# Spreading the norm factors of a token pair by a DRAM store and a repeating load instead of by products

## The chip, the cores and the metric

The kernel runs on one core of one Trainium2 chip. The metric is the device time of one execution in microseconds (us), from launch to end. Before the change the median of three runs is 1037.97 us (1037.33 to 1039.09).

The engines are named as in the profile: PE is TensorE, DVE is VectorE, ACT is ScalarE, POOL is GpSimd, SP is SyncE, which here only issues DMAs. POOL can issue DMAs too; they form a queue of their own (q0 in the page of the profile, beside q1 of SP).

## What is computed

One layer of a hybrid decoder, for 2048 prompt tokens and 8 sample tokens of width 1024:

```python
def rmsnorm(x, g):
    y = x * lax.rsqrt(jnp.mean(x * x, axis=-1, keepdims=True) + NORM_EPS)
    return y * g

h = rmsnorm(x, norm_g)
p = h @ w_in                      # (tokens, 1024) @ (1024, 8 * 512)
rq, rk, rv, rg, hq, hf, hi, hgate = jnp.split(p, 8, axis=-1)
...                               # retention heads, HGRN2 heads, gates
y = x + concat(o_ret, o_hg) @ w_out
out = rmsnorm(y, final_norm_g)
```

All of it is float32. What matters here is the first line of the layer: each token's row of `x` is scaled by one number, its norm factor `rsqrt(mean(x*x) + eps)`. The kernel holds `x` transposed, with the 1024 features on the partitions and tokens along the free axis. There a token's factor has to stand on every partition, as a row, to be multiplied in.

## The kernel before, in words

The 2048 tokens are cut into 8 pairs of two 128-token chunks. The products of the first part (`v_pair`, line 393) go over the pairs three times, once for each set of weight columns (values, then rq and gates, then rk and gates). The list `TOK` (line 199) gives the pair of each of the 24 steps: 4, 5, 6, 7, 2, 3, 0, 1 in the first set, then 1, 2, 4, 5, 3, 6, 7, 0, then 0 to 7. Steps 0 and 1 are done in another way: plain products on unscaled tokens, scaled by the norm factors when they leave PSUM (`plain_out`, line 635, ACT, where the factor stands on the token's partition and needs no spreading). From step 2 on a pair is multiplied by seven products of sums of blocks (a Strassen-Winograd scheme, `CHAIN`, line 364), each of 12 matmuls 128x128 by 128x512 in a high and low split; a step is 84 such matmuls.

For step i, `tok_ops(i)` (line 306) makes the operands:
- eight DVE instructions (line 313) multiply the raw tokens `xr` by `norm_g` and by the spread factors, `spread_to[i]`, a tile of 128 partitions by 256 tokens named `rb`
- ACT and DVE split them into high and low parts (`hi_lo`, lines 115 and 116, tiles `ab_h` and `ab_l`)
- DVE forms the sums S1 to S4 (lines 328 to 331), which `s_split` splits (tiles such as `s20h`).
- The scaled tokens and sums are stored to DRAM (`a_dram`, `s_dram`). Later steps on the same pair read them back ("spooled"). Only steps 2 to 7, 10 and 11 scale raw tokens, because pairs 4 and 5, of the plain steps, are scaled when they come again.

The factors come from `stats`: `stats_load` (line 257) loads the untransposed tokens into tiles `xn` (two buffers, 256 KB each, on SP's queue), `stats_sum` (line 263) squares and sums them on ACT (line 267, four a pair), and `stats_end` (line 275) has POOL add the partial sums (line 277) and raise to -0.5 (lines 111 and 112) into `rs_all`, which has a chunk's 128 factors in one column, one on each partition.

Spreading is by product. `spread_dg(i)` (line 284) has DVE multiply the identity by each of the two columns (line 288, tile `dg`), `spread(i)` (line 290) has PE multiply an all-ones matrix by each of these diagonal matrices (line 293, PSUM tile `prs`; each of the two products shows as two matmuls in the trace) and DVE copy the result to `rb` (line 295). The sample tokens do the same on a small scale: `decode_dg` (line 620), `decode_spread` (line 623, tiles `prsd` and `rbd`), and a DVE instruction (line 628) that scales the sample tokens `xs`, which sit in the tile `pk`.

The order on PE is that of the program, written out by hand: `after[n]` lists what is issued behind product n of step i, `after[n - 0.5]` in its middle. On the other engines and in the queues of SP and POOL a list scheduler orders the instructions by its own estimate of when each can start, and takes what comes first in the program where several could. `behind(f)` (line 124) ties the instructions of `f` behind the last ones of DVE, ACT and SP at that place; `past` (line 300) ties `spread_dg` behind the DVE instructions of the pair's `tok_ops`. All engines and queues work through their own lists in order, so that an instruction that waits holds up those behind it.

In the start of the kernel (lines 644 to 715) the weights are loaded and split, `stats(0)`, `stats(1)` and `stats(2)` run, `spread_dg(2)` and `spread(2)` surround the last plain products, `tok_ops(2)` follows and `stats(3)`. In the loop (line 918) step i handles the rest of `stats(i + 2)`: squares of the first half at `after[2]`, of the second half at `after[4]`, while `spread_dg(i + 1)` stands at `after[0]` and `spread(i + 1)` at `after[1]`. In the steps 2 to 5 `wg_load` also loads 1 MB of raw weights (`wgr`) for the next set, which PE multiplies by the sample tokens (`wg_decode`, line 531, `pgd`, line 600) and DVE sums (`w_sums`).

Of the kernel before, what the change touches and what calls it, by code (L numbers as in the profile page):

```python
# [18 lines left out]
P = 128  # L19
# [4 lines left out]
NB = 8  # L24
# [17 lines left out]
def step_kernel(ctx, tc, a, out):  # L42
# [24 lines left out]
    dg_dram = dr.tile([8, NB, P], F32, tag="dg_dram", name="dg_dram")  # L67
    a_dram = [dr.tile([P, KT, 2 * P], F32, tag=f"a_dram{p}", name=f"a_dram{p}") for p in range(8)]
    s_dram = [dr.tile([2, P, 2, 4, P], F32, tag=f"s_dram{p}", name=f"s_dram{p}") for p in range(8)]
    w_sums_dram = [  # L70
        {op: dr.tile([P, 4, GW], F32, tag=f"ws{n}{op}", name=f"ws{n}{op}") for op in ("T1", "T2", "T3", "T4")}
        for n in range(3)
# [173 lines left out]
    def spooled(i):  # L246
        return i >= 2 * N_V or (i >= N_V and TOK[i] not in TOK[:2])
# [27 lines left out]
    def stats_end(i):  # L275
        p, ms = V_ORDER[i], st[i]
        pool.tensor_tensor(ms[:, 0:2], ms[:, 0:2], ms[:, 2:4], op=ALU.add)
        rsqrt_mean(rs_all[:, 2 * p : 2 * p + 2], ms[:, 0:2], D, EPS)

    spread_to = {}  # L280

    dgs = {}

    def spread_dg(i):
        t = vq.tile([P, GW], F32, tag="rk", name=f"dg{i}")
        dgs[i] = [t[:, :P], t[:, P : 2 * P]]
        for dg, c in zip(dgs[i], (2 * TOK[i], 2 * TOK[i] + 1)):
            dve.tensor_scalar(dg, ident, rs_all[:, c : c + 1], None, op0=ALU.mult)

    def spread(i):  # L290
        pt = ps_tr.tile([P, 2, P], F32, tag="tr", name=f"prs{i}")
        for j, dg in enumerate(dgs[i]):
            pe.matmul(pt[:, j], ones, dg, start=True, stop=True)
        dst = vq.tile([P, GW], F32, tag="rq", name=f"rb{i}")[:, :256]
        dve.tensor_copy(dst, pt.rearrange("p a b -> p (a b)"))
        spread_to[i] = dst

    sop, lows = {}, {}

    def past(i, f):  # L300
        if i not in lows:
            return f()
        with tc.issue_after(lows[i]):
            f()

    def tok_ops(i, held=None):
        store = held.append if held is not None else lambda f: f()
        r0, r1 = xr[i]
        for j, r in enumerate((r0, r1)):
            if not spooled(i):  # L310
                for k in range(4):
                    kk = 4 * j + k
                    dve.scalar_tensor_tensor(  # L313
                        r[:, k], r[:, k], g_in[:, kk : kk + 1], spread_to[i], op0=ALU.mult, op1=ALU.mult
                    )
# [8 lines left out]
        lows[i] = next(x for x in reversed(nc.cur_bb.bb.instructions) if x.engine == dve.engine)  # L324
# [293 lines left out]
    dgd = sm.tile([NB, NB], F32, tag="dgd", name="dgd", bufs=1)  # L618

    def decode_dg():  # L620
        dve.tensor_scalar(dgd, ident[:NB, :NB], rsd[:, 1:2], None, op0=ALU.mult)

    def decode_spread():
        pt = ps_tr.tile([P, NB], F32, tag="tr", name="prsd")
        pe.matmul(pt, ones[:NB, :], dgd, start=True, stop=True)
        rb = sm.tile([P, NB], F32, tag="rbd", name="rbd", bufs=1)
        act.activation(rb, pt, AF.Copy)
        dve.tensor_tensor(xs, xs, rb.unsqueeze(1).to_broadcast([P, KT, NB]), op=ALU.mult)

    def x_decode():  # L630
# [37 lines left out]
            wv_split(k)  # L668
    for k in (0, 4, 2, 6):
        tok_load0(1, k)  # L670
    stats(1)
    stats(2)
    decode_inputs()
    for k in range(KT):
        x_split0(1, k)
# [242 lines left out]
    for i in range(2, n_tok):  # L918
# [13 lines left out]
        if same(i + 1):  # L932
            for op in ("S1", "S2", "S3", "S4"):
                sop[i + 1, op] = sop[i, op]
        elif i + 1 < n_tok:
            if not spooled(i + 1):
                after[0] += [lambda i=i: past(i, lambda: spread_dg(i + 1))]
                after[1] += [lambda i=i: spread(i + 1)]
            tied = behind if i >= N_V - 1 else lambda f: f()
            late = 2 if same(i) else 0  # L940
            after[2 + late] += [
                lambda i=i, t=tied: t(lambda: tok_ops(i + 1)), lambda i=i, t=tied: t(lambda: s_split(i + 1, 0))
            ]
            after[4 + late // 2] += [lambda i=i, t=tied: t(lambda: s_split(i + 1, 1))]
        if i + 2 < n_tok and not same(i + 2):
# [1042 lines left out]
```

## Time and profile before

| | before |
|---|---|
| median of 3 runs | 1037.97 us |
| profiled execution | 1038.73 us |
| its span | 1037.0 us |
| PE busy | 1023.4 us, 99% |
| DVE busy | 746.6 us, 72% |
| ACT busy | 556.5 us, 54% |
| POOL busy | 129.0 us, 12% |
| moved by DMA | 255.61 MB, mean 247 GB/s |
| POOL's DMA queue (q0) | 7440 packets, 24.76 MB |

In the lines of the profile, a time such as 84.37 is the start in us from the start of the span and the number behind it the duration; a name on the left of `<-` is written, those on the right are read. A matmul's duration overlaps with the next one's, so what a matmul costs is read from the distance between starts, which is 0.23 us in a dense row of 128x512 products. "PEld" is the weight load ahead of a matmul. In brackets stands how long the engine had been idle and what released it. The lines of waits give the sum, the number of times and the longest, in us.

### The profile page before, as it was taken

How to read it: one execution, taken by the hardware profiler on the slowest of the kernel's cores; microseconds unless marked ns; L12 is line 12 of the kernel's file. 1: busy time of each engine (PE TensorE's matmuls, PEld its weight loads, DVE VectorE, ACT ScalarE, POOL GpSimd, SP SyncE). 2: the span in 40 equal slices, each digit the busy share in tenths (PEclk: the TensorE clock that was granted, in tenths of full speed). 3: DMA queues.
4: the chain of work that ended last, by engine and by line, in shares of the span. 5: the costliest groups of instructions: out<-in, count | busy, mean ns of one | idle time of the engine just before them, and what ended most of it. 6: DMA issues, size and time to landing. Idle time of an engine off the chain costs nothing. (4 is left out here: it accounts for less than half of the span.)

```text
span 1037.0 us, 21324 instructions
## 1 busy us (share of the span) xinstructions
PE 1023.4 (99%) x8231; PEld 849.9 (82%) x8231; DVE 746.6 (72%) x1387; ACT 556.5 (54%) x1217; POOL 129.0 (12%) x231
## 2 busy tenths in 40 slices
PE   9999999999999999999999999999999999999997
PEld 7777778887778888888888889898888878888775
DVE  6886676887666876666665767768768577667886
ACT  7863346644445765545554756566656465433232
POOL 0310001000000111111111100111012102311122
PEclk9999999999999999999999999999999999999999
DMA  8699999779998975586885686745783395575652
GB/s 295 217 326 327 341 326 314 272 250 328 316 333 295 374 241 162 161 276 210 238 256 163 244 313 225 257 138 187 230 266 122 118 370 203 178 271 190 238 184 102
DMA packets 151270, 255.61 MB, mean 247 GB/s; under 512 B 11424, under 2 KB 79280, under 8 KB 151040
## 3 DMA queue, kind: packets, MB, share of 16 engines
q1 hardware_dynamic: 143584, 229.22, 65.6%
q0 software_dynamic: 7440, 24.76, 6.2%
q8 instruction: 65, 1.06, 0.4%
q14 instruction: 37, 0.30, 0.1%
q10 hardware_dynamic: 144, 0.26, 0.1%
HBM read 166.51 MB, written 87.69 MB: 245 GB/s over the span
## 5 line engine op out<-in xcount | busy, mean ns | idle before, releaser
L1235 ACT ACTIVATE kepth<-kh 128x1024 f32<-128x1024 f32 x24 | 25.5, 1061 | 70.4 <-DVE kh L1225 70.4
L1039 PE MATMUL pjfh<-xh,w_h 128*128 128x512 f32 (+2 forms) x160 | 59.5, 372 | 0.0
L1039 PE MATMUL pjqh<-xh,w_h 128*128 128x512 f32 (+2 forms) x160 | 59.0, 368 | 0.0
L1039 PE MATMUL pjqh<-xh,w_l 128*128 128x512 f32 (+2 forms) x160 | 55.7, 348 | 0.0
L1039 PE MATMUL pjfh<-xl,w_h 128*128 128x512 f32 (+2 forms) x160 | 55.7, 348 | 0.0
L1039 PE MATMUL pjqh<-xl,w_h 128*128 128x512 f32 (+2 forms) x160 | 55.6, 347 | 0.1
L1039 PE MATMUL pjfh<-xh,w_l 128*128 128x512 f32 (+2 forms) x160 | 55.6, 348 | 0.0
L1225 DVE TENSOR_TENSOR kh<-kh,fph 128x512 f32<-128x512 f32 x48 | 33.3, 695 | 23.0 <-PE plh L1255 13.2
L116 DVE TENSOR_TENSOR ab_l<-xr,ab_h 128x512 fp32r<-128x512 f32 (+1 forms) x40 | 37.5, 954 | 7.1 <-ACT ab_h L115 6.8
L782 DVE SCALAR_TENSOR_TENSOR obr<-por,omr,rg 128x128 f32<-128x128 f32 x64 | 18.0, 344 | 32.4 <-POOL omr L774 32.4
L772 ACT ACTIVATE obr<-por 128x128 f32<-128x128 f32 x64 | 16.9, 278 | 43.2 <-PE por L759 40.9
L115 ACT ACTIVATE ab_h<-xr 128x512 fp32r<-128x512 f32 (+1 forms) x40 | 32.4, 840 | 13.6 <-DVE xr L313 13.6
L419 ACT ACTIVATE vo<-vo 128x512 f32<-128x512 f32 x32 | 20.1, 630 | 27.3 <-DVE vo L413 13.4
L1039 PEld LDWEIGHTS pjqh<-xh,w_h 128*128 128x128 f32 x160 | 30.4, 190 | 4.6 <-issue 1.2
L1039 PEld LDWEIGHTS pjfh<-xh,w_h 128*128 128x128 f32 x160 | 30.2, 189 | 4.1 <-issue 0.4
L1039 PEld LDWEIGHTS pjqh<-xh,w_l 128*128 128x128 f32 x160 | 30.1, 188 | 4.2 <-issue 0.3
L1039 PEld LDWEIGHTS pjfh<-xh,w_l 128*128 128x128 f32 x160 | 30.1, 188 | 4.0
L1228 DVE TENSOR_TENSOR qqh<-qqh,fph 128x512 f32<-128x512 f32 x48 | 32.8, 684 | 0.0
L1039 PEld LDWEIGHTS pjqh<-xl,w_h 128*128 128x128 f32 x160 | 30.2, 189 | 2.9
L1039 PEld LDWEIGHTS pjfh<-xl,w_h 128*128 128x128 f32 x160 | 30.2, 189 | 2.7
L313 DVE SCALAR_TENSOR_TENSOR xr<-xr,g_in,rb 128x256 f32<-128x256 f32 x64 | 27.1, 480 | 7.1 <-issue 4.3
L1666 PE MATMUL py<-woh,oc_h 128*128 128x512 f32 x64 | 26.7, 417 | 0.0
(1840 smaller groups left out, 3383.1 us busy)
## 6 DMA issues: line engine op xcount, KB each, us to landing
xr<-a_dram SPq DMA_DIRECT2D x24, 512.0 KB, 5.2
S<-s_dram SPq DMA_DIRECT2D x24, 512.0 KB, 5.8
xn<-in_x_prompt SPq DMA_DIRECT2D x32, 256.0 KB, 3.5
xr<-in_x_t SPq DMA_DIRECT2D x16, 512.0 KB, 5.7
a_dram<-xr SPq DMA_DIRECT2D x16, 512.0 KB, 4.1
s_dram<-S SPq DMA_DIRECT2D x16, 512.0 KB
wgr<-in_w SPq DMA_DIRECT2D x16, 512.0 KB, 8.3
xr<-a_dram SPq DMA_DIRECT2D x32, 256.0 KB, 4.4
```

Source lines behind the costliest of these rows:

```text
L115: act.activation(h, src, AF.Copy)
L116: dve.tensor_tensor(l, src, h.bitcast(F32), op=ALU.subtract)
L313: dve.scalar_tensor_tensor(r[:, k], r[:, k], g_in[:, kk : kk + 1], spread_to[i], op0=ALU.mult, op1=ALU.mult)
L419: act.activation(o, src, AF.Silu)
L772: act.activation(o[:, cc], po[:, h], AF.Square, scale=P ** -0.5, accum_out=ms[:, h : h + 1])
L782: dve.scalar_tensor_tensor(o[:, cc], po[:, h], ms[:, h : h + 1], rb_of[c, "g"][:, cc], op0=ALU.mult, op1=ALU.mult)
L1039: pe.matmul(ps, ww[:, kk], x[:, k, b0 : b0 + n], start=(k == 0 and i == 0), stop=(k == KT - 1 and i == 2),)
L1225: dve.tensor_tensor(kv[:, :, 0, :], kv[:, :, 0, :], two[:, :, 1:2].to_broadcast([P, nb, b]), op=ALU.mult)
L1228: dve.tensor_tensor(qv[:, :, 1, :], qv[:, :, 1, :], two[:, :, 0:1].to_broadcast([P, nb, b]), op=ALU.mult)
L1235: act.activation(ss[:, 512:], k[:, :HALF], AF.Copy)
L1666: pe.matmul(ps, o[:, kk], w[:, k % 4, i * 512 : (i + 1) * 512], start=(k == 0 and n == 0), stop=(k == KT - 1 and n == 2),)
```

## The change

- `stats_end` stores the pair's 256 factors to DRAM, `rs_dram`, by a DMA of POOL's queue. For a pair of step 2 or later it calls `spread(i)` at once.
- `spread(i)` becomes one DMA on POOL's queue, which reads the 1 KB of factors 128 times over and writes them to all partitions of `rb`. It needs no PE, no PSUM and no DVE. `spread_dg` is gone, the tiles of `rb` alternate between the buffers `rq` and `rk`.
- For steps 10 and 11, whose factors lie in DRAM since the start, `spread` is issued behind product 4 of the step two ahead.
- All `stats` move one pair ahead: step i handles `stats(i + 3)`, `stats(4)` is in the start, and `stats(2)` comes before `stats(1)`. Their number does not change.
- `decode_spread` becomes a store and a repeating load on POOL's queue as well. The scaling of the sample tokens is a function of its own, `decode_scale`.

```diff
@@ tensors
+    rs_dram = [dr.tile([2, P], F32, tag=f"rs_dram{p}", name=f"rs_dram{p}") for p in range(8)]
+    rsd_dram = dr.tile([1, NB], F32, tag="rsd_dram", name="rsd_dram")
@@ stats_end
         rsqrt_mean(rs_all[:, 2 * p : 2 * p + 2], ms[:, 0:2], D, EPS)
+        pool.dma_start(rs_dram[p].rearrange("c t -> t c"), rs_all[:, 2 * p : 2 * p + 2])
+        if i >= 2:
+            spread(i)
@@
-    def spread_dg(i):
-        t = vq.tile([P, GW], F32, tag="rk", name=f"dg{i}")
-        dgs[i] = [t[:, :P], t[:, P : 2 * P]]
-        for dg, c in zip(dgs[i], (2 * TOK[i], 2 * TOK[i] + 1)):
-            dve.tensor_scalar(dg, ident, rs_all[:, c : c + 1], None, op0=ALU.mult)
-
     def spread(i):
-        pt = ps_tr.tile([P, 2, P], F32, tag="tr", name=f"prs{i}")
-        for j, dg in enumerate(dgs[i]):
-            pe.matmul(pt[:, j], ones, dg, start=True, stop=True)
-        dst = vq.tile([P, GW], F32, tag="rq", name=f"rb{i}")[:, :256]
-        dve.tensor_copy(dst, pt.rearrange("p a b -> p (a b)"))
+        dst = vq.tile([P, GW], F32, tag=("rq", "rk")[i % 2], name=f"rb{i}")[:, :256]
+        pool.dma_start(dst, rs_dram[TOK[i]].rearrange("c t -> (c t)").partition_broadcast(P))
         spread_to[i] = dst
@@ sample tokens
-    def decode_dg():
-        dve.tensor_scalar(dgd, ident[:NB, :NB], rsd[:, 1:2], None, op0=ALU.mult)
-
     def decode_spread():
-        pt = ps_tr.tile([P, NB], F32, tag="tr", name="prsd")
-        pe.matmul(pt, ones[:NB, :], dgd, start=True, stop=True)
         rb = sm.tile([P, NB], F32, tag="rbd", name="rbd", bufs=1)
-        act.activation(rb, pt, AF.Copy)
+        pool.dma_start(rsd_dram.rearrange("o b -> b o"), rsd[:, 1:2])
+        pool.dma_start(rb, rsd_dram[0].partition_broadcast(P))
+        dec_rb.append(rb)
...
+    def decode_scale():
+        rb = dec_rb[0]
         dve.tensor_tensor(xs, xs, rb.unsqueeze(1).to_broadcast([P, KT, NB]), op=ALU.mult)
@@ start
+    stats(2)
     stats(1)
-    stats(2)
...
-    spread_dg(2)
...
             if (c, ty) == (0, 0):
-                spread(2)
                 held = []
                 tok_ops(2, held)
...
     s_split(2, 1)
-    stats_load(4, 0)
+    stats(4)
+    stats_load(5, 0)
@@ loop, step i
-            if not spooled(i + 1):
-                after[0] += [lambda i=i: past(i, lambda: spread_dg(i + 1))]
-                after[1] += [lambda i=i: spread(i + 1)]
...
+        if N_V <= i + 2 < 2 * N_V and not spooled(i + 2):
+            after[4] += [lambda i=i: spread(i + 2)]
-        if i + 2 < N_V:
-            after[1 if i == 2 else 2] += [lambda i=i: behind(lambda: stats_sum(i + 2, 0)), lambda i=i: stats_load(i + 2, 1)]
-            after[4] += [lambda i=i: behind(lambda: stats_sum(i + 2, 1)), lambda i=i: stats_end(i + 2)]
-            if i + 3 < N_V:
-                after[5] += [lambda i=i: stats_load(i + 3, 0)]
+        if i + 3 < N_V:
+            after[1 if i == 2 else 2] += [lambda i=i: behind(lambda: stats_sum(i + 3, 0)), lambda i=i: stats_load(i + 3, 1)]
+            after[4] += [lambda i=i: behind(lambda: stats_sum(i + 3, 1)), lambda i=i: stats_end(i + 3)]
+            if i + 4 < N_V:
+                after[5] += [lambda i=i: stats_load(i + 4, 0)]
...
         if i == 2:
             after[3] += [lambda: behind(decode_values_out)]
-            after[0] += [decode_dg]
-            after[2] += [decode_spread]
+            after[0] += [decode_spread]
+            after[2] += [decode_scale]
```

More of the change, by code (lines that the diff above doesn't have):

```diff
@@ L278, in stats_end @@
         rsqrt_mean(rs_all[:, 2 * p : 2 * p + 2], ms[:, 0:2], D, EPS)
+        pool.dma_start(rs_dram[p].rearrange("c t -> t c"), rs_all[:, 2 * p : 2 * p + 2])
+        if i >= 2:
+            spread(i)
     spread_to = {}
-    dgs = {}
-    def spread_dg(i):
-        t = vq.tile([P, GW], F32, tag="rk", name=f"dg{i}")
-        dgs[i] = [t[:, :P], t[:, P : 2 * P]]
-        for dg, c in zip(dgs[i], (2 * TOK[i], 2 * TOK[i] + 1)):
-            dve.tensor_scalar(dg, ident, rs_all[:, c : c + 1], None, op0=ALU.mult)
-    def spread(i):
-        pt = ps_tr.tile([P, 2, P], F32, tag="tr", name=f"prs{i}")
-        for j, dg in enumerate(dgs[i]):
-            pe.matmul(pt[:, j], ones, dg, start=True, stop=True)
-        dst = vq.tile([P, GW], F32, tag="rq", name=f"rb{i}")[:, :256]
-        dve.tensor_copy(dst, pt.rearrange("p a b -> p (a b)"))
-        spread_to[i] = dst
[L298 to L304, printed above, removed]
+    def spread(i):
+        dst = vq.tile([P, GW], F32, tag=("rq", "rk")[i % 2], name=f"rb{i}")[:, :256]
+        pool.dma_start(dst, rs_dram[TOK[i]].rearrange("c t -> (c t)").partition_broadcast(P))
+        spread_to[i] = dst
+    sop = {}
     def tok_ops(i, held=None):
@@ L323, in tok_ops @@
             return
-        lows[i] = next(x for x in reversed(nc.cur_bb.bb.instructions) if x.engine == dve.engine)
         a11, a21, a12, a22 = r0[:, :, :P], r0[:, :, P:], r1[:, :, :P], r1[:, :, P:]
@@ L616, in decode_values_out @@
             sp.dma_start(vd_dram[ty], t)
-    dgd = sm.tile([NB, NB], F32, tag="dgd", name="dgd", bufs=1)
-    def decode_dg():
-        dve.tensor_scalar(dgd, ident[:NB, :NB], rsd[:, 1:2], None, op0=ALU.mult)
     def decode_spread():
-        pt = ps_tr.tile([P, NB], F32, tag="tr", name="prsd")
-        pe.matmul(pt, ones[:NB, :], dgd, start=True, stop=True)
         rb = sm.tile([P, NB], F32, tag="rbd", name="rbd", bufs=1)
-        act.activation(rb, pt, AF.Copy)
+        pool.dma_start(rsd_dram.rearrange("o b -> b o"), rsd[:, 1:2])
+        pool.dma_start(rb, rsd_dram[0].partition_broadcast(P))
+        dec_rb.append(rb)
+    dec_rb = []
+    def decode_scale():
+        rb = dec_rb[0]
         dve.tensor_tensor(xs, xs, rb.unsqueeze(1).to_broadcast([P, KT, NB]), op=ALU.mult)
```

## The prediction, made before the result was known

> **What bounds the kernel now.** I read the page first, then the busy time by stage, then the PE rows around the removed products, then PE's waits, then the rows of the other engines between 34 and 64 us, where the first pair to be scaled is prepared.
>
> The page:
>
> ```profile
> span 1037.0 us, 21324 instructions
> PE 1023.4 (99%) x8231; PEld 849.9 (82%) x8231; DVE 746.6 (72%) x1387; ACT 556.5 (54%) x1217; POOL 129.0 (12%) x231
> ```
>
> PE is busy for all but 14 us. So an instruction that leaves PE's list shortens the kernel by what it took there, unless PE then waits at that place or soon behind it; and work taken off DVE or ACT is worth nothing by itself. The profiled execution took 1038.73 us for this span, so 1.73 us lie around it, which the change doesn't touch.
>
> The products that go, from a dense place (PE's rows in order of time):
>
> ```profile
> 84.37 0.61 PE L293 MATMUL prs<-dg,ones 128*128 128x128 f32 x4
> 84.74 0.47 PE L360 MATMUL pv3a<-T2h,s30h 128*128 128x512 f32 x1
> 85.05 0.39 PE L360 MATMUL pv3a<-T2l,s30h 128*128 128x512 f32 x1
> 85.28 0.40 PE L360 MATMUL pv3a<-T2h,s30l 128*128 128x512 f32 x1
> ...
> 66.35 0.38 PE L625 MATMUL prsd<-dgd,ones 8*128 8x8 f32 x2
> 66.66 0.50 PE L360 MATMUL pv2c<-T1h,s21h 128*128 128x512 f32 x1
> 67.00 0.40 PE L360 MATMUL pv2c<-T1l,s21h 128*128 128x512 f32 x1
> ```
>
> Starts of neighbouring 128x512 products lie 0.23 us apart (85.05 to 85.28). One spread holds PE from 84.37 to 84.74, 0.37 us, and the product behind it starts late by a further 0.31 - 0.23 = 0.08 us: 0.45 us for a spread. The sample tokens' spread costs 0.31 + (0.34 - 0.23) = 0.42 us.
>
> How many there are, by the groups of that line (a spread is four of them):
>
> ```profile
> L293 PE MATMUL prs<-dg,ones x32: 272/274/275, 49.9 to 227.9; 128*128 128x128 f32 x32
> ```
>
> So eight spreads, all before 228 us.
>
> Second, the places where PE stands still near them. In the rows of PE when the first scaled pair begins (`pv2a`):
>
> ```profile
> 55.60 0.39 PE L360 MATMUL pv<-wv_h,ab_l 128*128 128x512 f32 x1
> ...
> 57.61 0.39 PE L360 MATMUL pv2a<-wv_l,ab_h 128*128 128x512 f32 x1
> ...
> 59.68 0.39 PE L360 MATMUL pv2b<-wv_l,ab_h 128*128 128x512 f32 x1
> ...
> 60.64 0.40 PE L360 MATMUL pv2b<-wv_h,ab_h 128*128 128x512 f32 x1
> ...
> 62.71 0.61 PE L293 MATMUL prs<-dg,ones 128*128 128x128 f32 x4
> 63.42 0.50 PE L360 MATMUL pv2a<-T2h,s20h 128*128 128x512 f32 x1
> ```
>
> From 55.60 to 57.61 there are five starts, which take 1.14 us where nothing waits, so 0.87 us are lost; from 59.68 to 60.64 there are two, 0.50 us lost. Behind the spread at 62.71 the next product comes after 0.71 us and not 0.37, 0.34 us lost. PE waits here for the operands of step 2, 1.7 us in all. From PE's list of waits there is one more:
>
> ```profile
> PE pgd L600 <- DMA wgr<-in_w: 1.0, 2, 0.5
> ```
>
> Twice, 0.5 us each, the sample tokens' products wait for raw weights, in a stretch where the DMA engines are full (busy time by stage; behind the clock come the DMA engines' busy share and GB/s):
>
> ```profile
> 64.00:85.00 21.00, 21.00 (x106) 16.49 (x105) 16.14 (x30) 9.74 (x20) 1.84 (x3) 1.00 0.99 371
> 85.00:107.00 22.00, 21.51 (x108) 16.80 (x108) 16.00 (x28) 9.06 (x17) 1.08 (x3) 1.00 0.96 334
> 107.00:128.00 21.00, 21.00 (x107) 16.56 (x106) 15.16 (x27) 9.29 (x17) 1.08 (x3) 1.00 0.98 343
> 128.00:150.00 22.00, 21.51 (x108) 16.87 (x107) 15.07 (x26) 9.25 (x17) 1.08 (x3) 1.00 0.95 343
> ```
>
> **The change part by part.** *Products removed:* 8 x 0.45 + 0.42 = 4.0 us off PE.
>
> *What of it comes back as waiting.* The spread at 62.71 stands in front of a wait: if the operand `s20h` and the freed bank come no sooner, PE only waits 0.45 us longer there. In the full DMA stretch PE comes to `pgd` sooner by each spread left out, while the weights come when DMA brings them; of the two places that wait, I count one as giving its 0.45 us back. (The second lies in step 5, which loses its 1 MB of `xn`, since all squares are one step earlier; that relief is worth more than the 128 KB that a repeating load adds.) That makes 4.0 - 0.9 = 3.1 us.
>
> *The way of the factors for step 2.* This is what is new and tight. POOL's rows, and the DVE and ACT rows that follow from them:
>
> ```profile
> 34.57 4.94 POOL L277 TENSOR_TENSOR ms<-ms 128x2 f32<-128x2 f32 x1 [6.81 <-ACT xn L267]
> ...
> 39.87 0.71 POOL L112 TENSOR_TENSOR rs_all<-rs_all,mhalf 128x2 f32<-128x2 f32 x1
> ...
> 56.39 1.18 POOL L112 TENSOR_TENSOR rs_all<-rs_all,mhalf 128x2 f32<-128x2 f32 x1
> ```
>
> ```profile
> 50.54 0.42 DVE L295 COPY rb<-prs 128x256 f32<-128x256 f32 x1 [1.79 <-PE prs L293]
> 51.00 2.47 DVE L313 SCALAR_TENSOR_TENSOR xr<-xr,g_in,rb 128x256 f32<-128x256 f32 x6
> ```
>
> ```profile
> 55.02 0.63 ACT L267 ACTIVATE xn<-xn 128x512 f32<-128x512 f32 x1 [1.36 <-DMA xn<-in_x_prompt]
> ...
> 55.65 0.61 ACT L115 ACTIVATE ab_h<-xr 128x512 fp32r<-128x512 f32 x1
> ```
>
> Before, `rb` of step 2 is there at 50.96, because PE reaches the spread so late. After, `stats(2)` takes the slot of `stats(1)`, whose factors are ready at 39.87 + 0.71 = 40.58. Then come a store and a repeating load. Neither is in this trace; the nearest rows are POOL's DMA issues and the times to landing:
>
> ```profile
> L575 POOL DMA_DIRECT2D T1l<-ws1T x2: 540/540/540, 171.9 to 173.2; - x2
> ```
>
> ```profile
> d_dram<-de POOLq DMA_DIRECT2D x8, 2.0 KB, 1.9
> ...
> o_dram<-obr POOLq DMA_DIRECT2D x16, 256.0 KB, 4.5
> ...
> out_new_hgrn_prompt<-S POOLq DMA_DIRECT2D x4, 64.0 KB, 3.0
> ...
> do<-d_dram POOLq DMA_DIRECT2D x1, 32.0 KB, 5.8
> ...
> dv<-vd_dram SPq DMA_DIRECT2D x8, 512.0 KB, 8.7
> ```
>
> The store moves 1 KB in pieces of 4 bytes. It is nearest to the 2 KB one in size, to the 256 KB one in the number of pieces: 1.9 to 4.5, I take 3.2. The load writes 128 KB; the only load by POOL from a small DRAM tensor took 5.8, a POOL store of 64 KB 3.0, and the repeating load that SP issues, of four times the size, 8.7. I take 5.8, the row nearest in kind, and the other two for bounds. With two issues of 0.54: 40.58 + 0.54 + 3.2 + 0.54 + 5.8 = 50.7, bounds 46.6 and 54.9. So the factors come about when they came before. Six scalings take 2.47 us, so four, which the first `ab_h` needs, 1.65. That `ab_h` started at 55.65, not because of DVE but because ACT stood before a square that waited for `xn`. Up to `rb` at 55.65 - 1.65 = 54.0 nothing changes; behind that each us is lost on PE, so the upper bound costs 0.9. The lower one can win the 1.7 us of waiting, if ACT's list lets `ab_h` ahead of the squares. I take zero.
>
> [...]
>
> *The wait on POOL's queue.* The load waits for the store to land, and behind it in POOL's list stand the adds and powers of `stats(1)`, whose factors `plain_out` uses on ACT. If they slip by 2 to 3 us, so does an emptying of PSUM whose bank PE needs again only for `pv2b`, seen at 59.68, which is a cover of over 10 us: nothing for PE; ACT's squares behind it wait for `xn` anyway.
>
> *Later steps.* Step 3's factors are ready at 57.57, by the same 10.1 us its `rb` is there at 67.7, the first `ab_h` could run at 69.4, and PE needs it only behind step 2's last product:
>
> ```profile
> 76.21 0.39 PE L360 MATMUL pv2a<-T4h,ab_h 128*128 128x512 f32 x1
> ```
>
> Seven us are left. From step 4 on the factors are a whole step earlier, 84 products of 0.23 us. Steps 10 and 11 have them in DRAM. Cost zero. The 9 stores and 9 loads are POOL time at 12% busy; DVE loses the diagonals, the copies and its waits for factors, ACT keeps its 32 squares. Zero each.
>
> *Sum:* -3.1 us. The profiled execution would be 1035.6; it lies 0.76 above the median of the runs, so the median goes from 1037.97 to 1034.9. A difference of 0.2%, 2.1 us, is about what can be told from none here (the three runs lie within 1.8). The forecast has bounds of -2.2 (upper bound of `rb`) and -4.0 (nothing comes back).
>
> **The rivals.** *First: the start clears too.* `rb` comes at 47 to 48, DVE is free then, and the first `ab_h` goes ahead of the late squares. Then the 1.7 us of waiting and the 0.45 at 62.71 are won: -3.1 - 2.1 = -5.2, 1032.8. For it: nothing ties `rb` to PE any more. Against: the 5.8 row, and ACT's order.
>
> *Second: DMA holds the pace from step 2 to 5.* The spreads of steps 2 to 5, the one at 62.71 among them, each stand ahead of a `pgd`. If all four times 0.45 end as waits for weights, 4.0 - 1.8 = 2.2 is left; with the 0.35 us of DMA time that 128 KB take at 371 GB/s added at the two places that wait already, 1.5: 1036.5. For it: the two `pgd` waits. Against: PE waits nowhere else there.
>
> *Third, on the other side: squares in front of the first operands on ACT.* The start has `stats(4)` whole, untied, where its first half used to be tied behind step 2. A square costs:
>
> ```profile
> L267 ACT ACTIVATE xn<-xn x32: 612/620/633, 17.4 to 144.0; 128x512 f32<-128x512 f32 x32
> L267 ACT ACTIVATION_READ_ACCUMULATOR xn<-xn x32: 184/187/191, 17.9 to 144.5; 128x1 f32 x32
> ```
>
> ```profile
> ACT xn L267 <- DMA xn<-in_x_prompt: 5.3, 7, 1.4
> ```
>
> That is 0.81 of work and 5.3 / 7 = 0.76 of waiting for `xn`, 1.57 us. Four squares before 55.65 already make PE wait. Two more ahead of step 2's splits cancel the gain (-3.1 + 3.1: 1038.0), four turn it to +3.2: 1041.2. It decides from two on. For it: the scheduler fills ACT's gaps by its own guess of when `xn` lands. Against: in the program `stats(4)` stands behind step 2's splits.
>
> *Fourth: POOL is held up by DVE.* The add at 34.57 took 4.94 us, the median of its line is 0.22:
>
> ```profile
> L277 POOL TENSOR_TENSOR ms<-ms x8: 195/224/4942, 24.8 to 144.8; 128x2 f32<-128x2 f32 x8
> ```
>
> DVE ran two-input instructions without a gap all that time. If the two DMA issues are held as long, `rb` comes 2 x 4.7 later, at 60.1, 6.1 us past the 54.0: -3.1 + 6.1 = +3.0, 1041.0; from 57.1 on the gain is gone. [...] Against it for DMAs: the issues of line 575 took 0.54 us.
>
> **How the numbers follow.** Forecast 0.42; start clears 0.17; DMA holds the pace 0.19; squares in front 0.09 with two, 0.07 with four; POOL held up 0.06. Faster by over 0.2%: 0.42 + 0.17 = 0.59. Within: 0.19 + 0.09 = 0.28. Slower: 0.07 + 0.06 = 0.13. The time is the forecast's, 1034.9. The range leaves out the two slower cases (0.13) and the far end of the first rival: 1032.3 to 1038.9. The faster cases alone span 1032.3 to 1035.8.
>
> **What would show it.** Right: no line with `prs` or `prsd`; PE busy lower by 3 to 4 us; the POOL queue up by 18 transfers; the first scaling of step 2 near 51; PE waits before `pv2a` and `pv2b` of 1 to 2 us. The first rival shows as these waits gone, the second as `pgd` waits of over 2 us, the third as squares waiting for `xn` ahead of `ab_h` and `s20h`, the fourth as long POOL issues between 40 and 50. The forecast is wrong if PE loses more than 3 us before 64, or if any later step waits for `rb`.

## The result, and the profile after

The changed kernel takes 1107.8 us (median of 4 runs, 1105.0 to 1113.0) against 1037.7 for the kernel before (four runs): a ratio of 1.067 (95% interval 1.064 to 1.069), 70 us slower. The forecast was 1034.9 with a range to 1038.9; direction and size are both wrong. The profiled execution took 1109.16 us.

The page of the changed kernel; PE's busy share, the granted clock (PEclk), both in tenths, and GB/s are given for 40 equal slices of the span:

```profile
span 1107.4 us, 21244 instructions
...
PE 1042.6 (94%) x8197; PEld 855.4 (77%) x8197; DVE 741.4 (67%) x1362; ACT 557.2 (50%) x1216; POOL 139.3 (13%) x249
...
PE   9946489999999999999999998999999999999997
...
PEclk9967889999999999999999998999999999999999
...
GB/s 289 144 164 181 152 347 266 279 371 170 313 316 332 313 337 277 176 176 242 213 226 263 157 269 249 200 279 160 137 290 175 154 222 320 97 342 157 242 174 96
...
q0 software_dynamic: 8144, 25.82, 6.8%
```

The clock and GB/s of the kernel before:

```profile
PEclk9999999999999999999999999999999999999999
...
GB/s 295 217 326 327 341 326 314 272 250 328 316 333 295 374 241 162 161 276 210 238 256 163 244 313 225 257 138 187 230 266 122 118 370 203 178 271 190 238 184 102
```

From the second to the fifth slice (28 to 138 us) the DMA engines moved about half as much as before, and from the third to the sixth, in which PE was busy for four to eight tenths, the granted clock was six to eight tenths. PE's busy time did not fall by 4 us, it rose by 19: the same matmuls ran longer. The start of each step on PE shows how much was lost where (min/median/max ns, then the first and last start in us). The changed kernel:

```profile
L347 PE MATMUL pv2a<-wv_h,ab_h x4: 392/628/793, 63.1 to 66.7; 128*128 128x512 f32 x4
...
L347 PE MATMUL pv3a<-wv_h,ab_h x4: 395/396/396, 111.8 to 113.9; 128*128 128x512 f32 x4
...
L347 PE MATMUL pv4a<-wv_h,ab_h x4: 395/396/396, 155.6 to 157.7; 128*128 128x512 f32 x4
...
L347 PE MATMUL pv5a<-wv_h,ab_h x4: 395/396/396, 179.7 to 181.8; 128*128 128x512 f32 x4
```

The kernel before:

```profile
L360 PE MATMUL pv2a<-wv_h,ab_h x4: 389/391/497, 56.3 to 58.8; 128*128 128x512 f32 x4
...
L360 PE MATMUL pv3a<-wv_h,ab_h x4: 389/389/389, 78.9 to 81.0; 128*128 128x512 f32 x4
...
L360 PE MATMUL pv4a<-wv_h,ab_h x4: 389/389/389, 100.4 to 102.4; 128*128 128x512 f32 x4
...
L360 PE MATMUL pv5a<-wv_h,ab_h x4: 389/389/389, 121.2 to 123.2; 128*128 128x512 f32 x4
```

Step 2 starts 7 us late, step 3 by 33, step 4 by 55, step 5 by 58.5. The rest, some 12 us, comes later. The rows also show a second thing: the undisturbed matmul takes 396 ns instead of 389.

Why the steps start late is seen on POOL. In the changed kernel line 281 is the store, line 289 the repeating load, line 114 the power that ends the making of the factors:

```profile
42.15 1.20 POOL L114 TENSOR_TENSOR rs_all<-rs_all,mhalf 128x2 f32<-128x2 f32 x1
43.65 0.79 POOL L281 DMA_DIRECT2D rs_dram<-rs_all  x1 [0.30 <-POOL rs_all L114]
54.05 0.58 POOL L289 DMA_DIRECT2D rb<-rs_dram  x1 [9.62 <-DMA rs_dram<-rs_all]
...
88.14 0.72 POOL L114 TENSOR_TENSOR rs_all<-rs_all,mhalf 128x2 f32<-128x2 f32 x1
89.27 0.80 POOL L281 DMA_DIRECT2D rs_dram<-rs_all  x1 [0.41 <-POOL rs_all L114]
99.55 0.57 POOL L289 DMA_DIRECT2D rb<-rs_dram  x1 [9.48 <-DMA rs_dram<-rs_all]
```

POOL waits 9.6 us for a store of 1 KB, and 9.5 for the next that it reads back. The first scaling of steps 2, 3 and 4 on DVE follows:

```profile
60.09 0.88 DVE L301 SCALAR_TENSOR_TENSOR xr<-xr,g_in,rb 128x256 f32<-128x256 f32 x2
...
103.86 2.46 DVE L301 SCALAR_TENSOR_TENSOR xr<-xr,g_in,rb 128x256 f32<-128x256 f32 x6 [19.57 <-DMA rb<-rs_dram]
...
133.92 2.46 DVE L301 SCALAR_TENSOR_TENSOR xr<-xr,g_in,rb 128x256 f32<-128x256 f32 x6 [16.12 <-DMA rb<-rs_dram]
```

Steps 3 and 4 wait for `rb`. At step 2 `rb` had landed at about 58 (54.05 and 3.9 to landing), and DVE came to the scaling late from a wait for a split on ACT, which in its turn had stood 1.33 us for the factors of pair 1.

And the DMA issues (KB each, median us to landing); the `xn` loads took 3.5 us before:

```profile
xn<-in_x_prompt SPq DMA_DIRECT2D x32, 256.0 KB, 8.9
...
rb<-rs_dram POOLq DMA_DIRECT2D x8, 128.0 KB, 6.1
...
rs_dram<-rs_all POOLq DMA_DIRECT2D x8, 1.0 KB, 10.2
```

So the repeating load costs what was thought (6.1 for 5.8, single ones from 3.3 to 10.1), and the store three times as much (10.2 for 3.2). That alone would make `rb` late. But `xn` is loaded by another queue, and the change added nothing to those loads: what made them land 5 us later?

### The profile page after: what moved, and what is told of

Same layout as the page of the kernel before. It is cut to its first block, busy times and chain, and to the rows that moved or that the text cites. A ratio compares the mean times of both kernels' runs of the same rounds, so it can differ in the third digit from the quotient of the medians.

```text
span 1107.4 us, 21244 instructions
## 1 busy us (share of the span) xinstructions
PE 1042.6 (94%) x8197; PEld 855.4 (77%) x8197; DVE 741.4 (67%) x1362; ACT 557.2 (50%) x1216; POOL 139.3 (13%) x249
## 4 chain that ended last, share of the span: by engine, by line
PE 61%; DMA 4%; DVE 3%; ACT 1%; issue 1%; SPq 0%; POOLq 0%; POOL 0%; ACTq 0%
PE po L347 11%; PE pjfh L1024 7%; PE pjqh L1024 7%; PE py L1651 4%; PE plh L1240 1%; PE par L730 1%; PE pur L737 1%; PE por L743 1%; PE por L745 1%; DMA or<-o_dram 1%; PE puh L1111 1%; PE poh L1127 1%; PE pv21a L347 1%; PE pv22a L347 1%; PE pv19a L347 1%; PE pv16a L347 1%
## 5 line engine op out<-in xcount | busy, mean ns | idle before, releaser
L768 DVE SCALAR_TENSOR_TENSOR obr<-por,omr,rg 128x128 f32<-128x128 f32 x64 | 18.0, 344 | 32.5 <-POOL omr L760 27.8
L269 ACT ACTIVATE xn<-xn 128x512 f32<-128x512 f32 x32 | 19.9, 624 | 34.2 <-DMA xn<-in_x_prompt 34.1
```

Of the source, the lines that this page charges most:

```text
L269: act.activation(r, r, AF.Square, accum_out=st[i][:, 2 * h + j : 2 * h + j + 1])
L768: dve.scalar_tensor_tensor(o[:, cc], po[:, h], ms[:, h : h + 1], rb_of[c, "g"][:, cc], op0=ALU.mult, op1=ALU.mult)
```

## The experiments

**The theories.** Theory 1: the store in 256 pieces of 4 bytes takes about 10 us and holds up every other transfer meanwhile. Rival A: the new order of the squares. Rival B: the repeating load of 128 KB. A third theory came with the 396 ns: where the operands lie. Each run's ratio is to the kernel before, run on the same chip, with its 95% interval. "Pair n" here and in the expectations is the pair of step n. Where rows of the input or of ones are spread, the expectation says so; their times are of the same work with other numbers.

**The stores alone** (e2): the kernel before plus the stores, which nothing reads. The order of the instructions on SP, ACT and DVE stays that of before, line for line; this holds for e5, e7, e8, e11, e13 and e16 as well.

```diff
 rsqrt_mean(rs_all[:, 2 * p : 2 * p + 2], ms[:, 0:2], D, EPS)
+pool.dma_start(rs_dram[p].rearrange("c t -> t c"), rs_all[:, 2 * p : 2 * p + 2])
```

> The kernel before, with one addition: the eight 1 KB stores in 256 pieces of 4 B, right behind each pair's factors on GpSimd. Nothing reads them; products, squares and their order stay as they were. Theory 1: 40 to 70 us slower than before (1078 to 1108), the xn loads at 8 to 9 us to landing, and a wait of ScalarE for xn of 5 us and more behind each early store. Rivals A and B: 1037 to 1040, since the order stays and there is no repeating load; nothing waits for the stores.

Measured: 1078.1 us, ratio 1.039 (1.037 to 1.041), +40 us. Its DMA issues:

```profile
xn<-in_x_prompt SPq DMA_DIRECT2D x32, 256.0 KB, 8.7
...
rs_dram<-rs_all POOLq DMA_DIRECT2D x8, 1.0 KB, 11.1
```

Theory 1 holds: stores that nothing waits for cost 40 us and bring the slow `xn` loads with them. How they do it shows in the busy share of the DMA engines (in tenths) and the rate in 40 slices of 0.325 us from 43 to 56 us. The store is issued at 43.28 and landed 11.2 us later:

```profile
DMA  7899989569679999990019593093955064033222
GB/s 202 309 384 347 347 265 240 151 227 252 277 235 271 366 297 189 88 32 0 0 44 50 25 25 13 0 25 13 32 13 13 0 22 13 32 13 25 25 22 19
```

From 48.5 us on all queues together move up to 50 GB/s, until past the landing at 54.5, although two `xn` loads issued at 45.53 are in flight and the DMA engines are busy for some four tenths of that time.

**What in the store is dear** (e7, e8, e11): again the kernel before plus stores that nothing reads. e7 writes 128 pieces of 8 B into 1 KB; e8 the 256 pieces of 4 B, each into 512 B of its own; e11 each 64 B from the next. Of each store only the target is shown, with its shape behind it:

```diff
-rs_dram[p].rearrange("c t -> t c")                    # e2: [2, P]
+rs_dram[p]                                            # e7: [P, 2]
+rs_dram[p].rearrange("c t o -> t c o")[:, :, 0:1]     # e8: [2, P, 128]
+rs_dram[p].rearrange("c t o -> t c o")[:, :, 0:1]     # e11: [2, P, 16]
```

> The kernel before plus the eight stores alone, nothing reads them, but in the order token, column: 128 pieces of 8 B, one after another in 1 KB of memory, in place of 256 pieces of 4 B in two rows. If a store costs by its pieces: half of the 40 us of the kernel with the 4-byte stores, 1055 to 1062, landing 5 to 6 us. If it costs by the start or the queue: 1075 to 1080 as there, landing 10 to 11. If only writes that jump between two rows are dear: 1037 to 1040.

> The kernel before plus the eight stores alone, nothing reads them, in 256 pieces of 4 B, but each piece in a 512 B line of its own (128 KB of memory for each store) in place of 1 KB for all. If the price is of many pieces written into the same line: 1037 to 1042, landing 2 to 4 us. If it is of the number of pieces: 1074 to 1082 as with the packed 4-byte stores, landing 10 to 11 us.

> The kernel before plus the eight stores alone, nothing reads them, in 256 pieces of 4 B that start 64 B apart (8 pieces in each 512 B line, 16 KB for each store). If what is dear is pieces that share 64 B: 1037 to 1041, as with a 512 B line for each. If what is dear is pieces that share 512 B, and the price goes with how many do: 8 in place of 128 to a line, 1040 to 1045. If packing did not matter below 512 B: 1075 and more, as with the packed ones.

Measured: e7 1049.3 us, 1.010 (1.006 to 1.014), landing 7.8; e8 1039.0, 1.000 (0.998 to 1.002), landing 4.5; e11 1036.8, 0.9985 (0.996 to 1.0005), landing 4.5. The DMA issues of e8, with as many starts, pieces and bytes as e2:

```profile
xn<-in_x_prompt SPq DMA_DIRECT2D x32, 256.0 KB, 3.6
...
rs_dram<-rs_all POOLq DMA_DIRECT2D x8, 1.0 KB, 4.5
```

So it is neither the number of pieces nor GpSimd's queue. It is small pieces packed side by side in DRAM: with 16 pieces in each 64 B the stores cost 40 us, with 8 they cost 10, with one nothing that can be told. e7 came out between its expected ranges; it has half as many pieces of twice the size as well, so that the price follows how many share 64 B is argued. Distances between 4 and 64 B were not tried with pieces of 4 B.

**The store in two large pieces** (e1):

```diff
-pool.dma_start(rs_dram[p].rearrange("c t -> t c"), rs_all[:, 2 * p : 2 * p + 2])
+pool.dma_start(rs_dram[p], ones[0:2, :])
...                                                   # sample tokens
-pool.dma_start(rsd_dram.rearrange("o b -> b o"), rsd[:, 1:2])
+pool.dma_start(rsd_dram, ones[0:1, :NB])
```

> The changed kernel, but each store writes the two rows of ones as 2 pieces of 512 B (the sample tokens' store 1 piece of 32 B) in place of 256 pieces of 4 B (8 of 4 B); its place, its queue, the repeating loads and the earlier squares stay. Left out: the factors, since rows of 1.0 are spread in their place. Theory 1 (the store in 4-byte pieces takes some 10 us and holds up every other transfer meanwhile): the loss goes; 1033 to 1037 us, the xn loads land in about 3.5 us again (8.9 in the changed kernel) and the load of rb for step 2 has landed by 51 us. Rival A (the earlier squares): 1095 to 1110. Rival B (the repeating load of 128 KB): 1095 to 1110.

Measured: 1062.4 us, 1.024 (1.022 to 1.026). 45 of the 70 us are gone and the `xn` loads land in 3.9 us, but 24 are left, which theory 1 doesn't have. (Stores of ones wait for no factors, so all of them were issued in the first 11 us, and the first two repeating loads with them, at 7.2 and 9.1 us, not in their old place.) The other parts had to be looked at.

**The order of the squares alone** (e3): the kernel before, products and all, with the moves of `stats` in the diff of the change.

> The kernel before with the changed order of the squares alone (pair 2's ahead of pair 1's, pair 4's ahead of step 2, each later pair's one step sooner); the products still spread the factors, no store, no repeating load. Theory 1: within 3 us of before, 1036 to 1041. Rival A: 1090 to 1108. Rival B: as theory 1.

Measured: 1047.7 us, 1.009 (1.007 to 1.011), +9.5 us: neither theory 1's 3 us nor rival A's 50. PE's rows say where:

```profile
L360 PE MATMUL pv2a<-wv_h,ab_h x4: 390/394/497, 57.5 to 60.0; 128*128 128x512 f32 x4
...
L360 PE MATMUL pv3a<-wv_h,ab_h x4: 389/389/390, 82.6 to 84.6; 128*128 128x512 f32 x4
...
L360 PE MATMUL pv4a<-wv_h,ab_h x4: 389/390/390, 109.5 to 111.6; 128*128 128x512 f32 x4
```

Step 2 takes 25.1 us for 22.6, step 3 26.9 for 21.5. In step 2 six `xn` loads are issued (two each at 63.65, 72.44 and 78.43 us) where there were two (at 65.39), 1 MB more in a stretch where the DMA engines were nearly full before (a busy share of 0.99 from 64 to 85 us). Step 3 has no more of them than before, but PE waits 3.3 us for `wgr` there (at 99 and 101 us), and the granted clock from 85 to 110 us is 0.86. That the loads brought forward are what delays `wgr` is argued.

**Where the operands lie** (e5, e12). The tile `dgd` of 32 B went with the products, so the tiles allocated behind it start 32 B lower. e5 makes the kernel before do just that, e12 gives the changed kernel an unused tile in `dgd`'s place.

```diff
-const.tile([P, 168], F32, name="fill")                               # e5, from before
+const.tile([P, 160], F32, name="fill")
+dgd = sm.tile([NB, NB], F32, tag="dgd", name="dgd", bufs=1)          # e12, from after
```

> The kernel before with one edit: the unused tile fill is 160 in place of 168 columns wide, so that every tile allocated after it, the moving operands wv_h, wv_l, xr, s20h among them, starts 32 B lower in each partition, as in the changed kernel, where the tile dgd (32 B) is gone. No instruction differs. Theory 3 (placement: moving operands that start 32 B past a multiple of 64 B cost the 389 to 396 ns per matmul that the profiles differ by): the matmul of 128x512 into pv from step 0 on takes 395 to 396 ns, and the kernel 1043 to 1048 us. Rival (the 396 ns come from a throttled clock after the early idle time of PE, or from the repeating loads): 389 ns, 1037 to 1039.

> The changed kernel plus one unused tile of 32 B in the place of dgd, so that the moving operands start where they did in the kernel before; no instruction differs. If the placement adds to the rest: matmul into pv 389 ns in place of 396, and 1107.8 - 8.3 = 1097 to 1101. If the waiting for the stores covers it: 1105 to 1110.

Measured: e5 1047.2 us, 1.009 (1.006 to 1.012), +9 us without one instruction changed. e12 1102.1 us, 1.061 (1.056 to 1.067), 5.7 below the changed kernel, though the two intervals overlap. PE's rows of step 5 in e5:

```profile
L360 PE MATMUL pv5a<-wv_h,ab_h x4: 395/396/396, 123.2 to 125.3; 128*128 128x512 f32 x4
...
L360 PE MATMUL pv5a<-T3h,s50h x4: 389/389/389, 134.7 to 136.7; 128*128 128x512 f32 x4
L360 PE MATMUL pv5a<-T4h,ab_h x4: 392/395/396, 141.4 to 143.5; 128*128 128x512 f32 x4
```

and in e12:

```profile
L347 PE MATMUL pv5a<-wv_h,ab_h x4: 389/389/389, 179.8 to 181.8; 128*128 128x512 f32 x4
```

The placement decides between 389 and 396 ns. It is not the start of the weights alone: in e5 the products of the first part that pay have `ab_h` or `ab_l` as their other operand (those with `wv` and `T4`, and with `B22` in steps 0 and 1, medians 395 to 396). Those with `T1`, `T2` and `T3`, and with `B22` beside the sums of steps 2 and later, have medians at most 1 ns above those before. The program takes `ab_h` and `ab_l` from a pool at the other end of the memory (`side="right"`), so the author's guess is that the 32 B count as a distance between the two operands; no run shows it.

**The repeating load** (e13, e16): the kernel before plus eight repeating loads that nothing reads.

```diff
+pool.dma_start(fill, a["x_prompt"][0, i, :168].partition_broadcast(P))    # e13
+with tc.issue_after(last_pool()):                                        # e16: behind the
+    pool.dma_start(...)                                                   # pair's factors
```

> The kernel before plus eight repeating loads on GpSimd's queue that nothing reads (168 floats of an input row to all 128 partitions, 86 KB each, into the unused tile fill), each right behind its pair's factors; the products stay, and the order of the instructions on SP, ScalarE and VectorE is that of the kernel before, line for line. If the loads themselves cost some 11 us at 128 KB: 1044 to 1048 (two thirds of it at 86 KB). If it was the order that the scheduler made: 1038 to 1041.

> The kernel before plus eight repeating loads that nothing reads (84 KB each, 168 floats of an input row to all partitions, into the unused tile fill), each tied on GpSimd behind the instruction that makes its pair's factors, so that none is issued at the start of the kernel. The order on SP, ScalarE and VectorE is that of the kernel before, line for line. If loads at that place cost nothing: 1037 to 1040. If the 4.7 us of the run with the loads at the start (1043.4) are the loads' own: 1042 to 1045.

Measured: e13 1043.4 us, 1.005 (1.003 to 1.007). But nothing tied these loads, and the scheduler issued all eight in the first 38 us, among the first weights: in the profiled run the factors of pair 0 came 10 us late (37.4 for 27.8). e16 has them at their place: 1040.2 us, 1.001 (0.999 to 1.003). At 84 KB a load costs nothing that can be told, so rival B falls as the cause of tens of us; a load of the full 128 KB was not tried in this way.

**Loads in place of the products** (e9, e10, e14; e17, e18 with tied loads). `spread(i)` is a repeating load of an input row; products, diagonals and copies are gone, there is no store. e10 and e18 have the new order of the squares, e14 keeps the products for pairs 2 and 3.

```diff
-pe.matmul(pt[:, j], ones, dg, start=True, stop=True)
-dve.tensor_copy(dst, pt.rearrange("p a b -> p (a b)"))
+pool.dma_start(dst, a["x_prompt"][0, i, :256].partition_broadcast(P))     # e9, e10, e14
+with tc.issue_after(last_pool()):                                        # e17, e18
+    pool.dma_start(...)
```

> The kernel before with its own order of the squares and its own placement; the sixteen products of the spreads and VectorE's diagonal tiles are gone, and each rb is a repeating load of 128 KB on GpSimd's queue right behind its pair's factors, out of a row of the input, so that it waits for no store. The sample tokens' spread stays a product. Left out: the factors, since the row that is spread is another. If the repeating loads cost nothing, the forecast's own sum without the way of the factors: 1038.8 - 8 x 0.45 = 1035, at most 1037. If they cost the 10 us that the kernel with the two-row stores has over order and placement (1062.4 - 1047.7 - 8.3 + 3.6): 1043 to 1047.

> As the kernel with the repeating loads alone, but with the changed order of the squares. Left out: the factors. Sum of parts: 1047.7 (order alone) - 3.6 = 1044 if the loads are free; 1053 to 1057 if they cost some 10 us; and if order and loads only cost together (free alone, dear here), the run with the loads alone stays at 1035 and this one is at 1053 or more.

> The kernel before with its products for pairs 2 and 3, and repeating loads of 128 KB out of an input row in place of the products for the other six spreads. Left out: the factors of those six. SP's order stays that of before up to step 7, ScalarE's but for three places in step 3. If the order at the start is what cost: 1038.8 - 6 x 0.45 = 1036, between 1034 and 1038. If the loads: six eighths of 11 less 2.7, 1043 to 1046.

> The kernel with the repeating loads alone in place of the products (old squares, old placement), each load of 128 KB now tied behind its pair's factors on GpSimd. Left out: the factors, since rows of the input are spread. If the early issue was all that cost there: 1035 to 1037, below the kernel before. If the order that the scheduler makes without the products costs (pair 2's splits ahead of pair 3's squares on ScalarE, pair 3's xn loads behind the stores of pair 2 on SP): 1040 to 1047, with VectorE or PE waiting for xr and wgr in steps 2 and 3.

> As the one with the tied loads in place of the products, with the changed kernel's order of the squares. Left out: the factors. This is the changed kernel without any store and without the sample tokens' way over DRAM, at the old placement. By e3 (order alone, 1047.7) less 3.6 for the products: 1044; if order and loads hurt each other as in e10: 1049 to 1053. What the changed kernel at the old placement (1102.1) has above this run is the stores and what waits for them: 49 to 58 us.

Measured: e9 1047.1 us, 1.007 (1.005 to 1.010); e10 1050.5, 1.013 (1.009 to 1.017); e14 1045.1, 1.007 (1.0045 to 1.009); e17 1059.8, 1.021 (1.018 to 1.024); e18 1052.7, 1.014 (1.011 to 1.017). None reaches the 1035 of a free spread. In e9 and e10 the first two loads went out at 1.5 us, untied, which blurs them. e17, above both of its expected ranges, is clean in this and shows where the time goes. SP's issues in e17:

```profile
56.04 0.88 SPq L240 DMA_DIRECT2D xr<-in_x_t  x2
57.02 1.05 SPq L329 DMA_DIRECT2D s_dram<-S  x2
58.13 1.26 SPq L261 DMA_DIRECT2D xn<-in_x_prompt  x1
...
60.30 0.86 SPq L261 DMA_DIRECT2D xn<-in_x_prompt  x1
61.22 0.64 SPq L522 DMA_DIRECT2D wgr<-in_w  x1
68.43 0.33 SPq L261 DMA_DIRECT2D xn<-in_x_prompt  x1
68.81 0.43 SPq L522 DMA_DIRECT2D wgr<-in_w  x1
```

and in the kernel before:

```profile
53.68 0.33 SPq L261 DMA_DIRECT2D xn<-in_x_prompt  x1
...
55.77 0.33 SPq L261 DMA_DIRECT2D xn<-in_x_prompt  x1
...
59.90 0.88 SPq L240 DMA_DIRECT2D xr<-in_x_t  x2
60.88 1.12 SPq L334 DMA_DIRECT2D s_dram<-S  x2
62.05 1.84 SPq L527 DMA_DIRECT2D wgr<-in_w  x2
```

Without the products pair 2's splits stand ahead of pair 3's squares on ACT, and so two `xn` loads behind 2 MB of `xr` and `s_dram`. ACT waits for them:

```profile
67.69 0.63 ACT L267 ACTIVATE xn<-xn 128x512 f32<-128x512 f32 x1 [7.58 <-DMA xn<-in_x_prompt]
```

Pair 3's factors are ready at 69.76 instead of 57.57, and DVE's first scaling of step 3 runs at 75.88:

```profile
75.88 2.86 DVE L308 SCALAR_TENSOR_TENSOR xr<-xr,g_in,rb 128x256 f32<-128x256 f32 x7 [5.41 <-DMA rb<-in_x_prompt]
```

In the kernel before it ran at 65.52. The order has changed, that is shown; the likely reason, that the list scheduler estimates `rb` as ready earlier when no work on PE stands before it, is not. e14 lies where its expectation put the case that loads of 128 KB cost (1043 to 1046), not at 1036. In its profiled run, the fastest of the eight (1041.6), step 3 takes 23.4 us for 21.4, with 2.9 us of waiting for `wgr`, and step 8 22.0 for 20.4, with 1.7 for the weights `B22l`. Whether the full-size loads do this or the order stays open: rival B is out for the 70 us, but not for some 7 of them.

**Versions that might have won** (e4, e6, e15). DVE turns the factors by a 32x32 transpose (0.21 us in e4), so that a pair is stored as two starts of four pieces of 128 B, with the true factors. e4 has the new order and the new placement; e6 the old order but for pair 2, and the old placement; e15 keeps the products for pairs 2, 3 and 4.

```diff
+dve.transpose(rs_t, rs_all)
+for c in range(2):
+    pool.dma_start(rs_dram[p][c].rearrange("(b t) -> b t", b=4), rs_t[2 * p + c :: 32])
```

> The changed kernel, but VectorE first turns the factors by a 32x32 transpose (one instruction of 128x32 for each pair, about 0.1 to 0.2 us), so that each store is 2 starts of 4 pieces of 128 B (8 pieces in place of 256); GpSimd issues one start more for each pair. Repeating loads and earlier squares stay, and the factors are the true ones. Theory 1: 1033 to 1037, the two stores land in 2 to 4 us each, rb for step 2 landed by 52 us. Rival A or B: 1095 and more. If stores by the GpSimd queue as such hold up the other transfers, whatever their pieces: 1100 and more here and in the kernel that stores two rows.

> Stores in 128 B pieces behind VectorE's transpose as in the kernel that turned the factors, but with the old order of the squares (only pair 2's ahead of pair 1's is kept), the turn and the store one start after each pair's factors, and an unused tile of 32 B in dgd's place, so that all moving operands start where they did before. Sum by the runs so far: 1065 less 7 to 9 (placement), less 5 to 9 (order) = 1047 to 1053 if the repeating loads themselves cost some 10 us; 1034 to 1039 if they cost nothing and the order and placement are all that was left. Matmul 389 ns either way.

> A version that might beat both, with the true factors: products for pairs 2, 3 and 4 as before; for the other five spreads VectorE's 32x32 transpose, two stores of 4 pieces of 128 B for each pair and a repeating load; old order of the squares, operands where they were. If the way over DRAM (store 5 us, load 4 us, turn and issues 3 us) fits into the step between factors and scaling: 1038.8 - 5 x 0.45 = 1036.5, 1035 to 1038. If the factors of pairs 5 to 7 come late, as they did with the old order and all pairs over DRAM: 1042 to 1060.

Measured: e4 1065.2 us, 1.027 (1.025 to 1.029); e6 1075.4, 1.036 (1.0325 to 1.0395); e15 1059.7, 1.021 (1.0185 to 1.024). The stores land in 5.0 to 6.1 us and the `xn` loads in 3.6 to 4.2, so the hold-up is gone. But e4 is 28 us above the range of theory 1, and e6 above both of its ranges. The way over DRAM, turn, issues, store and load, takes 8 to 15 us (in e6 from the end of the power to the first scaling), and with the old order of the squares it does not fit behind the factors: DVE waits 49.3 us for `rb` in e6 and 15.2 in e4. DVE's waits in e15:

```profile
DVE xr L330 <- DMA rb<-rs_dram: 31.4, 3, 11.7
```

The early squares that would give it room cost 9.5 us themselves. At most the 4 us of products could be won, and none of these versions beats the kernel before; e11, the lowest median, is the kernel before with idle stores and can't be told from it.

## Why the prediction was wrong, point by point

**The sum of the 70 us by the runs.** New order and loads for products, no stores, old placement: +14.6 (e18). Stores, the waits for them and the sample tokens' way over DRAM: 1102.1 - 1052.7 = 49 (e12 over e18); stores that nothing waits for cost 40 in the kernel before (e2). Placement: 5.7 in the changed kernel (after over e12), 8 to 9 by itself (e5). What the sample tokens' store costs alone was not tried.

**The step that failed.** "The way of the factors" took the store at 3.2 us with bounds of 1.9 and 4.5, from a row that was near in bytes and one that was near in the number of pieces. It was 10.2. Neither row had the property that costs: small pieces packed side by side (11.1 us to landing in e2, 4.5 for as many pieces 64 or 512 B apart). And the store's price was put down as its own delay alone. It was paid by the other transfers in flight, as the `xn` loads show (8.9 us to landing for 3.5), and so the factors were late at their source too: 43.35 for 40.58, `rb` at about 58 (54.05 and 3.9 to landing) for 50.7 with an upper bound of 54.9. (The load's 5.8 was right as a median, but its row was not the only one of its kind: `dgt<-dg_dram`, also 32 KB, took 5.7.)

**The wait on POOL's queue.** A slip of 2 to 3 us was counted for the factors of pair 1, and nothing for PE. They were ready at 58.21, behind squares that waited for `xn` (in the kernel before, the third power, whose place they took, ended at 45.75), and the emptying of PSUM on ACT that waited for them stood ahead of a split that DVE needed before step 2's first scaling.

**The later steps.** "Seven us are left" for step 3 assumed its factors at 57.57. They came at 88.86: ACT's squares waited 8.71 and 3.28 us for held-up `xn` loads, the later of which stood on SP's queue behind a store that waited for the late sums of step 2. POOL itself was idle for 12.68 us before them. The prediction's own sign of error, a later step that waits for `rb`, is there with 19.6 and 16.1 us.

**The products.** 0.45 us for each spread holds. Where nothing else disturbs, in e18 at the old placement, step 6 takes 19.04 us for 19.54 before, step 9 20.06 for 20.55; step 7, without a spread, takes 19.04 in both. The gain exists and is buried.

**The rivals.** The third, squares in front, was the right place, the start and the order of the squares, with too small a price: 3 or 6 us forecast, 9.5 measured for the order alone; it counted ACT's work and not the 1 MB of loads that moved into a full stretch. Its sign is there in the changed kernel, where ACT stands before a square and the second `ab_h` of step 2 comes behind it, at 73.01, though the last scaling had ended at 64.55:

```profile
71.73 0.63 ACT L269 ACTIVATE xn<-xn 128x512 f32<-128x512 f32 x1 [8.71 <-DMA xn<-in_x_prompt]
```

PE's product `pv2b` then waits 6.5 us for that `ab_h`. The second, waits for `pgd`, grew to 5.9 us and was not what decided. The first did not happen: `rb` landed at about 58, not at 47 to 48. The fourth is refuted: the issues took 0.6 to 0.95 us; that DVE was what held POOL's add at 34.57 is not shown.

**What was in no step.** The removal of a 32 B tile, and that the order on ACT and SP changes when the products go.

**The price by size.** 1 KB in 256 pieces of 4 B landed in a median of 4.5 us where the pieces lie apart (e8 and e11; 3.0 and 2.9 for their third stores, issued at 46) and of 10.2 in the change; the load of 128 KB took 6.1. Neither bytes nor the number of pieces tell these stores apart. e8 and e11 show that pieces of 4 B cost the other transfers nothing that can be told as long as they lie 64 B apart or more (`xn` landed in 3.6 and 3.4 us, for 3.5 before). Why packed neighbours cost so much was not shown.

## What to carry to other kernels

Before a column of one number on each partition is stored to packed DRAM by a plain DMA, which cost 5.0 us a store here (e2), try to give each number 64 B (e11: nothing that can be told; a load that reads single numbers 64 B apart was not tried here), or to turn the column into rows first (e4: `xn` at 4.2 us), and look at the landing of other transfers, not only at the store's own. Before a tile is removed or resized, see that the operands of the hot matmuls keep their start (396 ns for 389 in e5), and compare the order of each engine's instructions before and after, since it may change far from the work that was removed, as in e17. A copy of the suspected operation beside the unchanged kernel, read by nobody, prices it in one run, if it is tied to its place.

## What the runs showed of the hardware that was not expected

- A DRAM store of 1 KB holds up the other queue's transfers, for 6 us and more in the stretch shown, when its small pieces lie side by side: 256 x 4 B packed land in 11.1 us and cost 5.0 us a store (40 / 8), 128 x 8 B in 7.8 us and 1.3, 256 x 4 B placed 64 or 512 B apart in 4.5 us and nothing that can be told.
- Moving tiles by 32 B made the 128x512 matmuls of the first part that read `ab_h` or `ab_l` take 396 ns instead of 389, 9 us in this kernel (e5).
- A wait on PE costs twice here: after the gap of 6.1 us ahead of step 2 the matmuls of the changed kernel took a median of 628 ns and started 0.43 us apart, for 0.23 in a dense row. The granted clock was 1.00 from 55 to 59.5 us and 0.50 from 59.5 to 66.3.
